# Modulation of layer 1 moved into the feed-forward, compression on shifted pairs in column strips, queries split once per half-row and copied by DMA

## The chip, the cores and the metric

The kernel runs on one core of a Trainium2 chip. The metric is the device time of one execution in microseconds; a time stands for the median of several runs. The profile is of one execution, whose span runs from its first to its last instruction.

## The reference, cut to what matters

Two layers over 1024 tokens of width 1024, float32. Each layer has a mixing sub-layer (four kinds of heads behind one input projection) and a feed-forward one; both are scaled and shifted by a modulation that depends on `c` alone.

```python
def reference(x, c, positions, ...):
    cond = jax.nn.silu(c)
    for l in range(DEPTH):
        mod = cond @ w_mod[l] + b_mod[l]
        sh1, sc1, gt1, sh2, sc2, gt2 = jnp.split(mod, N_MOD, axis=-1)
        h = rms_norm(x, norm_g[l, 0]) * (1.0 + sc1) + sh1
        y = mixer_block(h, positions, ...)
        x = x + gt1 * rms_norm(y, norm_g[l, 1])
        h = rms_norm(x, norm_g[l, 2]) * (1.0 + sc2) + sh2
        y = jnp.square(jax.nn.relu(h @ w_up[l])) @ w_down[l]
        x = x + gt2 * rms_norm(y, norm_g[l, 3])
    return x

# in the sparse attention of the mixer: 63 windows of 32 tokens, 16 apart, for keys (j=0) and values (j=1)
def compress(t, j):
    z = (t[:, blk] + cmp_pos[j]).reshape(B, n_cmp, CMP_BLOCK * HD)
    return jax.nn.silu(z @ cmp_w1[j]) @ cmp_w2[j]
```

The product `z @ w1` equals `t[blk] @ w1 + cmp_pos @ w1`, and the second term is the same for every window.

## The kernel before, in words

Tokens are worked on in two halves of T = 512, features on 128 partitions. The program calls, in this order: `mods_start` (load x, `cond` from c, the modulation j = 0 and 1 of layer 0), then for layer 0 `mix(0,0)`, `mix(0,1)`, `mods` for what is left, `ff(0,0)`, `mix(1,0)`, `ff(0,1)`, `mix(1,1)`, `ff(1,0)`, `ff(1,1)`. A scheduler reorders instructions within each engine by priority and readiness; the tail of a mixer half (residual and h2, under `tc.high_priority`) is put late. Every engine works its own list in order. All loads are issued by SP, in order, too.

**Matrix products.** A weight unit is 128x512 float32, 256 KB. It lands in a raw tile (`wraw`, L152), ACT casts it to the high part (L161), DVE subtracts to the low part (L125), and `mm3` (L167 to L169) makes three matmuls per 128 rows, 12 per unit. There are three lanes: `a` (3 raw tiles, 4 split ones), `b` (3 and 4) and `f` for the feed-forward (4 and 6, high and low each taking one). A feed-forward half has 128 units: `up` makes a hidden tile out of two (relu, square, split into `hid`), `down` one unit per output tile and group, summed into `y` by DVE (L131).

**Modulation.** `mod_col` takes one of 48 blocks of 128 outputs per layer: two 128x512 pieces of `w_mod` are loaded, each multiplied by `cond` and summed along the row by one DVE instruction with a read of its accumulator (L232), and both sums and the bias are added (L134). `mods_start` loads into 12 tiles `mw`; all the rest, 160 pieces, go through two tiles `mr` that belong to no stage, so the scheduler may place them anywhere from the first mixer on. Layer 0's j = 2 is due at the residual of `mix(0,0)`, j = 3 and 4 at its h2.

**Sparse attention** (`nsa_part`). `kvt` holds keys and values of the half with 16 columns of the half before. `compress` adds the positions into `zc` (8 DVE adds per call, L131), and multiplies by w1 in 32 matmuls (two passes each) that fill 32 of 128 output partitions (L650). A logistic chain on 32x256, two transposes and w2 give the compressed keys. Queries are rotated into `qr` and, for each block j of 128 tokens, split into a high and a low part (`qh`, L687, and `ql`, L125) that stand on both halves of the partitions: 4 casts and 4 subtractions. The scores (L744, L746) use them.

The GLA in the same mixer makes its state products on strips of 32 columns of the array:

```python
PE.matmul(kp[32 * hh:32 * hh + 32, j, :],
          k3t[64 * r:64 * r + 64, j, 32 * hh:32 * hh + 32],
          vtm[hh // 2][64 * r:64 * r + 64, j, 64 * (hh % 2):64 * (hh % 2) + 64],
          start=True, stop=True, tile_position=(64 * r, 32 * hh))
```

Of the kernel before, what the change touches and what calls it, by code (L numbers as in the profile page):

```python
# [7 lines left out]
F32 = mybir.dt.float32  # L8
# [8 lines left out]
DEPTH = 2  # L17
T = 512
# [17 lines left out]
def trunk_kernel(ctx, tc, xT, c, pos, freq, sel, w_in, conv_w, cmp_pos, cmp_w1, cmp_w2,  # L36
# [60 lines left out]
    par = []  # L97
    for l in range(DEPTH):
        d = {}
        for name, shape in (("ng", [128, 4, 8]), ("bmod", [128, 48]), ("conv", [128, 3, 2]),  # L100
                            ("pos", [128, 32]), ("gain", [128, 8]), ("mod", [128, 6, 8]),
                            ("A1", [128, 8]), ("G1", [128, 8]), ("A2", [128, 8]), ("G2", [128, 8])):
            d[name] = const.tile(shape, F32, name=f"{name}{l}")
        par.append(d)

    def load_params(l, names):
        src = {"ng": norm_g, "bmod": b_mod, "conv": conv_w, "pos": cmp_pos, "gain": gains}
        for n in names:
            dma(out=par[l][n], in_=src[n][l])

# [8 lines left out]
    cmp_halo = const.tile([128, 16], F32, name="cmp_halo")  # L119
# [108 lines left out]
    def mod_col(l, j, k, mk):  # L228
        mp = work.tile([128, 2], F32, name="mp", tag="mp", bufs=4)
        for kh in range(2):  # L230
            raw = mk(w_mod[l, 8 * j + k, :, kh * T:kh * T + T], [128, T])
            V.tensor_tensor_reduce(out=raw, in0=raw, in1=cond[kh], scale=1.0, scalar=0.0,  # L232
                                   op0=ALU.mult, op1=ALU.add, accum_out=mp[:, kh:kh + 1])
        stt(par[l]["mod"][:, j, k:k + 1], mp[:, 0:1], mp[:, 1:2], par[l]["bmod"][:, 8 * j + k:8 * j + k + 1],
            ALU.add, ALU.add)
# [332 lines left out]
    def nsa_part(l, hf, h, rg, gates):  # L568
# [65 lines left out]
        def compress():  # L634
            k4 = kvt.rearrange("p (a m r) -> p a m r", m=8, r=2)
            p4 = d["pos"].rearrange("p (b m r) -> p b m r", b=2, r=2)
            hid = ps("mm", (32, 2, 128))
            for jj in range(2):
                z = rg.tile([128, 16, 32], F32, name="zc", tag="P", bufs=3)
                rs = slice(64 * jj, 64 * jj + 64)  # L640
                for r in range(2):
                    for bb in range(2):
                        add(z[64 * r:64 * r + 64, 8 * bb:8 * bb + 8, :],
                            k4[rs, bb:bb + 32, :, r].rearrange("p a m -> p m a"),
                            p4[rs, bb, :, r:r + 1].to_broadcast([64, 8, 32]))
                for q in range(4):
                    w = bt((128, 4, 128))
                    dma(out=w, in_=cmp_w1[l, jj, :, 4 * q:4 * q + 4, :])
                    for m in range(4):
                        PE.matmul(hid[:, jj, :], z[:, 4 * q + m, :], w[:, m, :],  # L650
                                  start=(q == 0 and m == 0), stop=(q == 3 and m == 3))
            act = pt((32, 2, 128))
            logsig(act, hid, pt((32, 2, 128)))
            A.activation(act, act, AF.Exp)
            mul(act, act, hid)
# [21 lines left out]
        for j in range(4):  # L677
# [56 lines left out]
            # selected (every causal block) and window branches  # L734
# [59 lines left out]
            # compressed branch  # L794
# [39 lines left out]
    def mix(l, hf, h, between=None):  # L834
        d = par[l]
        gain = d["gain"]
        with ExitStack() as es:
            gr = es.enter_context(region("gates"))
            if l == 0 and hf == 0:
                sx = ("ff", "ff", "ff")  # L840
                with region("wb", "right") as lane_pool["b"]:
# [8 lines left out]
                    mods(0, (2, 3, 4))  # L850
# [32 lines left out]
    def ff(l, hf):  # L883
# [7 lines left out]
        def up(n):  # L891
# [9 lines left out]
            hid[n] = (hi, lo)  # L901

# [7 lines left out]
        def down(g, cs=slice(0, T), ws=None):  # L910
            for n in range(8):
# [151 lines left out]
```

## Time and profile before

| | |
|---|---|
| median of 3 runs | 2651.31 us (2650.48 to 2655.39) |
| profiled execution, span | 2656.2 us |
| PE busy | 2513.5 us, 95% |
| DVE busy | 1680.0 us, 63% |
| ACT busy | 1310.3 us, 49% |
| moved from and to HBM | 281.47 MB read, 17.83 MB written |
| mean granted clock of TensorE | 0.985 |

The span is 4.9 us above the median of the runs. PE is TensorE's matmuls, PEld its weight loads, DVE VectorE, ACT ScalarE, SP the engine that issues the DMAs. A share of busy time is a mean over all stages; a stage is read from its own stretch of the trace.

### The profile page before, as it was taken

The page shows a single profiled execution, that of the slowest core. Times are in us where ns is not written, and L with a number is a line of the kernel's source. Part 1 is how long each engine was busy: PE and PEld are TensorE (multiplying, and loading weights), DVE is VectorE, ACT ScalarE, POOL GpSimd, SP SyncE. Part 2 cuts the span into 40 slices and gives each one's busy share as a digit, 9 for nine tenths or more (in the row PEclk, how much of TensorE's full clock was granted, in tenths as well). Part 3 has the DMA queues.
Part 4 walks back from the last instruction along what each step waited for, and adds up shares of the span by engine and source line. Part 5 has one row for each costly group of instructions (what it writes and reads, how often), then busy time and mean ns, then how long its engine had stood idle before and what let it go on. Part 6 is the DMA issues. An engine that isn't in the chain of part 4 may idle for free.

```text
span 2656.2 us, 34273 instructions
## 1 busy us (share of the span) xinstructions
PE 2513.5 (95%) x11690; PEld 1989.3 (75%) x11690; DVE 1680.0 (63%) x3540; ACT 1310.3 (49%) x2649; POOL 56.5 (2%) x65
## 2 busy tenths in 40 slices
PE   2899879999999999999999999999999999999998
PEld 1676657677778887767788887777777888788887
DVE  7797987888574448457674446547876544534446
ACT  3474534468654345356653435345775443434343
POOL 0100000200000000010000000001000000000000
PEclk9999989999999999999999999999999999999999
DMA  7435566511343334222243334222123333533332
GB/s 270 138 97 174 192 204 202 179 53 36 100 142 98 96 99 143 82 71 69 95 144 100 96 97 145 88 61 89 40 76 121 98 96 99 179 97 98 96 99 84
DMA packets 168937, 301.56 MB, mean 114 GB/s; under 512 B 20453, under 2 KB 24122, under 8 KB 168762
## 3 DMA queue, kind: packets, MB, share of 16 engines
q1 hardware_dynamic: 168762, 299.37, 36.3%
q8 instruction: 92, 1.51, 0.2%
q14 instruction: 83, 0.68, 0.1%
HBM read 281.47 MB, written 17.83 MB: 113 GB/s over the span
## 4 chain that ended last, share of the span: by engine, by line
PE 76%; DVE 10%; ACT 4%; DMA 4%; issue 2%; POOL 0%; DVEq 0%; SPq 0%; ACTq 0%; POOLq 0%
PE ps_ff L168 16%; PE ps_ff L169 16%; PE ps_ff L167 16%; PE ps_mm L167 6%; PE ps_mm L169 6%; PE ps_mm L168 6%; DMA mr<-in_w_mod_dram 3%; PE ps_pv L705 1%; PE ps_pv L704 1%; DVE mr L232 1%; PE ps_mm L699 1%; ACT bp L754 1%; PE ps_t L189 1%; PE ps_s L744 1%; DVE w_a L125 1%
## 5 line engine op out<-in xcount | busy, mean ns | idle before, releaser
L161 ACT CAST w_f<-raw_f 128x512 fp32r<-128x512 f32 x504 | 313.3, 622 | 649.7 <-PE ps_ff L168 638.6
L125 DVE TENSOR_TENSOR w_f<-raw_f,w_f 128x512 fp32r<-128x512 f32 x504 | 348.7, 692 | 261.6 <-ACT w_f L161 254.7
L169 PE MATMUL ps_ff<-h,w_f 128*128 128x512 f32 x1024 | 405.9, 397 | 17.1 <-DVE w_f L125 17.1
L167 PE MATMUL ps_ff<-h,w_f 128*128 128x512 f32 x1024 | 404.8, 396 | 4.8 <-ACT h L203 4.8
L168 PE MATMUL ps_ff<-h,w_f 128*128 128x512 f32 x1024 | 406.6, 397 | 0.6 <-DVE h L134 0.4
L167 PE MATMUL ps_ff<-hid,w_f 128*128 128x512 f32 x992 | 388.9, 392 | 0.1
L168 PE MATMUL ps_ff<-hid,w_f 128*128 128x512 f32 x992 | 388.6, 392 | 0.0
L169 PE MATMUL ps_ff<-hid,w_f 128*128 128x512 f32 x992 | 388.2, 391 | 0.0
L167 PE MATMUL ps_mm<-h,w_a 128*128 128x512 f32 x832 | 336.4, 405 | 34.8 <-ACT w_a L161 30.5
L169 PE MATMUL ps_mm<-h,w_a 128*128 128x512 f32 x832 | 332.7, 400 | 11.7 <-DVE w_a L125 11.6
L168 PE MATMUL ps_mm<-h,w_a 128*128 128x512 f32 x832 | 338.8, 409 | 0.9 <-DVE h L125 0.9
L131 DVE TENSOR_TENSOR y<-y,ps_ff 128x512 f32<-128x512 f32 (+1 forms) x232 | 154.9, 668 | 238.0 <-PE ps_ff L169 237.1
L161 ACT CAST w_a<-raw_a 128x512 fp32r<-128x512 f32 x208 | 128.6, 618 | 233.0 <-PE ps_mm L168 216.2
L169 PEld LDWEIGHTS ps_ff<-h,w_f 128*128 128x128 f32 x1024 | 195.0, 190 | 60.1 <-DVE w_f L125 18.8
L125 DVE TENSOR_TENSOR w_a<-raw_a,w_a 128x512 fp32r<-128x512 f32 x208 | 143.3, 689 | 152.2 <-ACT w_a L161 146.0
L167 PEld LDWEIGHTS ps_ff<-h,w_f 128*128 128x128 f32 x1024 | 195.4, 191 | 47.6 <-ACT h L203 6.5
L168 PEld LDWEIGHTS ps_ff<-h,w_f 128*128 128x128 f32 x1024 | 195.0, 190 | 45.2 <-issue 2.7
L167 PEld LDWEIGHTS ps_mm<-h,w_a 128*128 128x128 f32 x832 | 158.0, 190 | 81.2 <-ACT w_a L161 33.6
L167 PEld LDWEIGHTS ps_ff<-hid,w_f 128*128 128x128 f32 x992 | 186.6, 188 | 40.5 <-issue 1.4
L168 PEld LDWEIGHTS ps_ff<-hid,w_f 128*128 128x128 f32 x992 | 186.7, 188 | 39.1 <-issue 1.0
L169 PEld LDWEIGHTS ps_ff<-hid,w_f 128*128 128x128 f32 x992 | 186.7, 188 | 37.8 <-issue 0.5
L169 PEld LDWEIGHTS ps_mm<-h,w_a 128*128 128x128 f32 x832 | 157.9, 190 | 55.8 <-DVE w_a L125 15.1
(350 smaller groups left out, 3586.4 us busy)
## 6 DMA issues: line engine op xcount, KB each, us to landing
raw_f<-in_w_up_dram SPq DMA_DIRECT2D x256, 256.0 KB, 2.7
raw_f<-in_w_down_dram SPq DMA_DIRECT2D x256, 256.0 KB, 2.6
mr<-in_w_mod_dram SPq DMA_DIRECT2D x160, 256.0 KB, 3.0
raw_a<-in_w_in_dram SPq DMA_DIRECT2D x144, 256.0 KB, 2.8
raw_a<-in_w_o_dram SPq DMA_DIRECT2D x64, 256.0 KB, 2.9
mw<-in_w_mod_dram SPq DMA_DIRECT2D x32, 256.0 KB, 4.4
bp<-in_cmp_w_dram SPq DMA_DIRECT2D x32, 256.0 KB, 4.6
raw_b<-in_w_in_dram SPq DMA_DIRECT2D x32, 256.0 KB, 3.0
```

The costliest lines, as they stand in the source:

```text
L125: V.tensor_tensor(out=out, in0=a, in1=b, op=ALU.subtract)
L131: eng.tensor_tensor(out=out, in0=a, in1=b, op=ALU.add)
L161: A.copy(hi, raw)
L167: PE.matmul(ps_ap, wh, xh, start=start, stop=False)
L168: PE.matmul(ps_ap, wh, xl, start=False, stop=False)
L169: PE.matmul(ps_ap, wl, xh, start=False, stop=stop)
L189: PE.matmul(p, ones, acc, start=True, stop=True)
L232: V.tensor_tensor_reduce(out=raw, in0=raw, in1=cond[kh], scale=1.0, scalar=0.0, op0=ALU.mult, op1=ALU.add, accum_out=mp[:, kh:kh + 1])
L699: PE.transpose(tp[0:kn, hh, :], cols(h0 + hh), ident)
L704: PE.matmul(pv[:, h0:h0 + nh, :], vst, th[0:kn], start=first[0], stop=False)
L705: PE.matmul(pv[:, h0:h0 + nh, :], vst, tl[0:kn], start=False, stop=last)
L744: PE.matmul(sp[:, 0:w], qh[:, h0 + hh, :], KX[:, 128 * k0:128 * k0 + w], start=True, stop=False)
```

## The change

Three things are done.

*Modulation.* `cond` becomes one 128x1024 tile, and a reduction may cover a whole block: `mod_dot` loads 512 KB and makes one 128x1024 reduction. The opening does 16 of these (6 tiles `mw`) and adds the bias for j = 0 and 1 at once. Layer 0's j = 2, 3, 4 stay in `mix(0,0)` as 48 pieces of 128x512 (`mod_half`), through the three raw tiles of lane `b`. The rest, 56 blocks, is handed to the feed-forward: `ff(0,0)` gets 48 and `ff(0,1)` 8, as steps that `up` and `down` call, with three tiles `mr` in a region `md` that lives as long as that feed-forward.

*Compression.* `kvt` holds two copies of each of keys and values, the second shifted by one token, on the two halves of the partitions, so that no `zc` is built. The 16 matmuls per part fill four strips of 32 columns in turn (`tile_position`), a matmul with `sel4` (four stacked 32x32 identities) sums the strips, and the positions' term is made once per layer in the same way and added on DVE. The logistic chain works on 128x64.

*Queries.* Each half-row of `qr` is split once, on its own partitions, and two DMAs per half (64 KB each) copy high and low part to the other half: 4 DMAs per block, 64 in all, on SP.

```diff
+    cond = const.tile([128, 1024], F32, name="cond")
+    def mod_dot(l, j, k, mk, acc):
+        raw = mk(w_mod[l, 8 * j + k], [128, 1024])
+        V.tensor_tensor_reduce(out=raw, in0=raw, in1=cond, scale=1.0, scalar=0.0,
+                               op0=ALU.mult, op1=ALU.add, accum_out=acc)
...
-                t = su.tile(shape, F32, name="mw", tag="mw", bufs=12)
+                t = su.tile(shape, F32, name="mw", tag="mw", bufs=6)
...
+                ma = work.tile([128, 2, 1], F32, name="ma", tag="ma", bufs=4)
                 for j in (0, 1):
-                    mod_col(0, j, k, mk)
+                    mod_dot(0, j, k, mk, ma[:, j, :])
+                add(par[0]["mod"][:, 0:2, k:k + 1], ma, bm[:, 0:2, k:k + 1])
...
-    def mods(l, js):
+    def mods_now(l, js, lane):
+        for j in js:
+            for k in range(8):
+                mod_half(l, j, k, lambda src, shape: wraw(lane, src, shape))
+            mod_scale(l, j, slice(0, 8))
+    def mods_steps(todo, pl):
         def mk(src, shape):
-            t = work.tile(shape, F32, name="mr", tag="mr", bufs=2)
+            t = pl.tile(shape, F32, name="mr", tag="mr", bufs=3)
             dma(out=t, in_=src)
             return t
-        for j in js:
+        for l, j in todo:
+            ma = work.tile([128, 8], F32, name="mv", tag="mv", bufs=2)
             for k in range(8):
-                mod_col(l, j, k, mk)
-            mod_scale(l, j, slice(0, 8))
+                mod_dot(l, j, k, mk, ma[:, k:k + 1])
+                if k == 7:
+                    add(par[l]["mod"][:, j, :], ma, par[l]["bmod"][:, 8 * j:8 * j + 8])
+                    mod_scale(l, j, slice(0, 8))
+                yield
...
-        kvt = rg.tile([128, 528], F32, name="kvt")
+        kvt = rg.tile([128, 2, 528], F32, name="kvt")
...
-        A.copy(kvt[:, 16:528], p)
+        for jj in range(2):
+            A.copy(kvt[0:64, jj, 16:528], p[64 * jj:64 * jj + 64])
+            V.tensor_copy(kvt[64:128, jj, 15:527], p[64 * jj:64 * jj + 64])
...
         def compress():
-            hid = ps("mm", (32, 2, 128))
-            for jj in range(2):
-                z = rg.tile([128, 16, 32], F32, name="zc", tag="P", bufs=3)
-                rs = slice(64 * jj, 64 * jj + 64)
-                for r in range(2):
-                    for bb in range(2):
-                        add(z[64 * r:64 * r + 64, 8 * bb:8 * bb + 8, :],
-                            k4[rs, bb:bb + 32, :, r].rearrange("p a m -> p m a"),
-                            p4[rs, bb, :, r:r + 1].to_broadcast([64, 8, 32]))
...
+            def partial(col):
+                hid = ps("mm", (128, 2, 128))
+                for jj in range(2):
+                    for i in range(16):
+                        c = i % 4
+                        PE.matmul(hid[32 * c:32 * c + 32, jj, :], col(jj, i), ws[4 * jj + i // 4][:, i % 4, :],
+                                  start=i < 4, stop=i >= 12, tile_position=(0, 32 * c))
+                hs = pt((128, 2, 128))
+                A.copy(hs, hid)
+                return hs
+            hx = partial(lambda jj, i: k5[:, jj, i // 8:i // 8 + 32, 2 * (i % 8)])
             hp_ = ps("mm", (128, 2, 32))
             for jj in range(2):
-                PE.transpose(hp_[:, jj, :], act[:, jj, :], ident[0:32, 0:32])
+                PE.matmul(hp_[:, jj, :], hx[:, jj, :], sel4, start=True, stop=True)
+            if hf == 0:
+                hb = partial(lambda jj, i: pos2[l][:, jj, 2 * i:2 * i + 32])
+                pb = ps("mm", (128, 2, 2))
+                for jj in range(2):
+                    PE.matmul(pb[:, jj, :], hb[:, jj, :], sel4[:, 0:2], start=True, stop=True)
+                A.copy(posb[l], pb[:, :, 0:1])
             hs = pt((128, 2, 32))
-            A.copy(hs, hp_)
+            add(hs, hp_, posb[l].to_broadcast([128, 2, 32]))
...
-                for o0 in (0, 64):
-                    V.tensor_copy(hv[o0:o0 + 64], qr[rs, :, tj])
-                for o0 in (0, 64):
-                    sub(lv[o0:o0 + 64], qr[rs, :, tj], hv[rs].bitcast(F32))
+                ro = slice(64 - 64 * r, 128 - 64 * r)
+                V.tensor_copy(hv[rs], qr[rs, :, tj])
+                sub(lv[rs], qr[rs, :, tj], hv[rs].bitcast(F32))
+                for v in (hv, lv):
+                    dma(out=v[ro].bitcast(F32), in_=v[rs].bitcast(F32))
...
-                    mods(0, (2, 3, 4))
+                    mods_now(0, (2, 3, 4), "b")
...
+    def ff(l, hf, todo=()):
+        if not todo:
+            return ff_body(l, hf, None)
+        with region("md") as rg:
+            steps = mods_steps(todo, rg)
+            y = ff_body(l, hf, lambda: next(steps, None))
...
             hid[n] = (hi, lo)
+            if step:
+                step()
...
                     add(y[n][:, cs], y[n][:, cs], p)
+                if step and n % 2:
+                    step()
...
-    mods(0, (5,))
-    mods(1, range(6))
-    xt = ff(0, 0)
+    xt = ff(0, 0, ((0, 5), (1, 1), (1, 0), (1, 2), (1, 4), (1, 3)))
...
-    xt = ff(0, 1)
+    xt = ff(0, 1, ((1, 5),))
```

**The order that comes out of it.** On SP in the tail of `mix(0,0)`, around the loads of the output projection's weights (`raw_a<-in_w_o`), before:

```order
L275 DMA mr<-in_w_mod_dram 128x512 x2
L152 DMA raw_f<-in_w_up_dram 128x512
L275 DMA mr<-in_w_mod_dram 128x512 x2
L152 DMA raw_a<-in_w_o_dram 128x512
L137 DMA xo<-in_xT_dram 128x512 x3
L152 DMA raw_a<-in_w_o_dram 128x512
L137 DMA xo<-in_xT_dram 128x512
L152 DMA raw_a<-in_w_o_dram 128x512
L275 DMA mr<-in_w_mod_dram 128x512 x2
L152 DMA raw_a<-in_w_o_dram 128x512
```

and now:

```order
L166 DMA raw_b<-in_w_in_dram 128x512 x11
L166 DMA raw_b<-in_w_mod_dram 128x512 x24
L151 DMA xo<-in_xT_dram 128x512
L166 DMA raw_a<-in_w_o_dram 128x512
L166 DMA raw_b<-in_w_mod_dram 128x512 x3
L166 DMA raw_a<-in_w_o_dram 128x512 x2
L166 DMA raw_b<-in_w_mod_dram 128x512 x3
L166 DMA raw_a<-in_w_o_dram 128x512
```

The loads of the modulation (`w_mod`) stood one or two at a time between the weight loads; now 24 in a row stand behind the last loads of lane `b` (`raw_b<-in_w_in`), and then threes between the weight loads. Five loads of `w_o` stand further up.

On SP in `ff(0,0)`, the loads of the feed-forward's weights (`raw_f`) before, of which there is nothing else in the list there:

```order
L152 DMA raw_f<-in_w_down_dram 128x512 x2
L152 DMA raw_f<-in_w_up_dram 128x512 x8
L152 DMA raw_f<-in_w_down_dram 128x512 x8
L152 DMA raw_f<-in_w_up_dram 128x512 x8
L152 DMA raw_f<-in_w_down_dram 128x512 x8
```

and now, a few units after the steps begin:

```order
L306 DMA mr<-in_w_mod_dram 128x1024 x3
L166 DMA raw_f<-in_w_up_dram 128x512
L306 DMA mr<-in_w_mod_dram 128x1024 x4
L166 DMA raw_f<-in_w_up_dram 128x512
L306 DMA mr<-in_w_mod_dram 128x1024 x3
L166 DMA raw_f<-in_w_up_dram 128x512
L306 DMA mr<-in_w_mod_dram 128x1024 x7
L166 DMA raw_f<-in_w_down_dram 128x512 x2
L306 DMA mr<-in_w_mod_dram 128x1024
```

Three to seven loads of 512 KB stand ahead of a weight load where none stood.

On DVE in `ff(0,0)`, before (`w_f` is a weight split, `y` the sum over groups, `hid` the split of a hidden tile):

```order
L125 TENSOR_TENSOR w_f<-raw_f,w_f 128x512
L131 TENSOR_TENSOR y<-y,ps_ff 128x512
L125 TENSOR_TENSOR w_f<-raw_f,w_f 128x512
L131 TENSOR_TENSOR y<-y,ps_ff 128x512
L125 TENSOR_TENSOR w_f<-raw_f,w_f 128x512
L125 TENSOR_TENSOR hid<-r,hid 128x512
L131 TENSOR_TENSOR y<-y,ps_ff 128x512
L125 TENSOR_TENSOR w_f<-raw_f,w_f 128x512 x3
```

and now (each `mr,mv` row is a 128x1024 reduction, the `mv` row behind it the read of its accumulator):

```order
L139 TENSOR_TENSOR w_f<-raw_f,w_f 128x512
L145 TENSOR_TENSOR mod_99<-mv,bmod_96 128x8
L247 ISA mr,mv<-mr,cond 128x1024
L247 ISA mv 128x1
L142 TENSOR_TENSOR G_103<-mod_99,ng_95 128x8
L139 TENSOR_TENSOR w_f<-raw_f,w_f 128x512 x2
L247 ISA mr,mv<-mr,cond 128x1024
L247 ISA mv 128x1
L247 ISA mr,mv<-mr,cond 128x1024
L247 ISA mv 128x1
L139 TENSOR_TENSOR w_f<-raw_f,w_f 128x512
```

One to three reductions stand ahead of each weight split. From the first of the 48 to the last the list holds 29 weight splits, and 30 of the reductions stand within the first 13 of these.

## Rows read from the trace of the kernel before

**Rows 1.** The first page: busy time by engine; shares of the last chain
```profile
PE 2513.5 (95%) x11690; PEld 1989.3 (75%) x11690; DVE 1680.0 (63%) x3540; ACT 1310.3 (49%) x2649; POOL 56.5 (2%) x65
...
PE 76%; DVE 10%; ACT 4%; DMA 4%; issue 2%; POOL 0%; DVEq 0%; SPq 0%; ACTq 0%; POOLq 0%
```

**Rows 2.** Table by stretch: length, busy by engine (count), clock, DMA share, GB/s
```profile
0.00:25.00 25.00, 2.07 (x2) 0.50 (x2) 17.85 (x54) 12.29 (x20) 1.50 (x9) 1.00 0.92 330
25.00:50.00 25.00, 1.02 (x3) 0.79 (x3) 24.50 (x73) 5.56 (x8) 0.00 (x0) 1.00 0.66 212
50.00:266.00 216.00, 201.30 (x1031) 149.62 (x1030) 172.20 (x512) 114.34 (x282) 13.48 (x14) 0.98 0.47 146
266.00:385.00 119.00, 95.27 (x355) 69.55 (x354) 107.61 (x232) 58.85 (x100) 0.72 (x1) 0.90 0.61 194
385.00:705.00 320.00, 305.47 (x1539) 231.65 (x1539) 259.54 (x659) 192.72 (x458) 13.86 (x13) 0.99 0.39 121
789.20:867.90 78.70, 78.70 (x349) 65.20 (x348) 33.25 (x51) 30.93 (x52) 0.00 (x0) 1.00 0.33 97
```

**Rows 3.** Timeline, DVE, opening: start, length, instruction
```profile
17.91 0.69 DVE L232 CUSTOM_DVE_ANT_0 mw<-mw,cond 128x512 f32<-128x512 f32 x1
18.52 0.22 DVE L134 SCALAR_TENSOR_TENSOR mod<-mp,bmod 128x1 f32<-128x1 f32 x1
18.65 0.69 DVE L232 CUSTOM_DVE_ANT_0 mw<-mw,cond 128x512 f32<-128x512 f32 x1
```

**Rows 4.** Groups by line and form: busy us, mean ns, idle before, its releaser
```profile
L232 DVE CUSTOM_DVE_ANT_0 mr<-mr,cond 128x512 f32<-128x512 f32 x160 | 110.6, 693 | 37.2 <-DMA mr<-in_w_mod_dram 36.6
...
L751 DVE CUSTOM_DVE_ANT_0 bp<-ps_s,cm 128x512 f32<-128x512 f32 x56 | 37.9, 685 | 2.6 <-PE ps_s L746 2.3
...
L650 PE MATMUL ps_mm<-bp,zc 128*32 128x128 f32 x256 | 31.4, 288 | 10.3 <-issue 10.3
...
L125 DVE TENSOR_TENSOR ql<-qr,qh 64x256 fp32r<-64x256 f32 x64 | 26.8, 418 | 1.4
...
L131 DVE TENSOR_TENSOR zc<-kvt,pos 64x256 f32<-64x256 f32 x32 | 22.9, 753 | 0.3
...
L687 DVE CAST qh<-qr 64x256 fp32r<-64x256 f32 x64 | 18.4, 288 | 2.3 <-PE ps_s L765 0.8 <-PE ps_s L744 0.3
...
L751 DVE CUSTOM_DVE_ANT_0 bp<-ps_s,cm 128x128 f32<-128x128 f32 x24 | 6.5, 285 | 3.0 <-PE ps_s L746 2.8
```

**Rows 5.** Instructions on mr in 50 to 266, 266 to 385, 385 to 705
```profile
L232 DVE CUSTOM_DVE_ANT_0 mr<-mr,cond x55: 647/686/1152, 82.2 to 265.7; 128x512 f32<-128x512 f32 x55
L232 DVE CUSTOM_DVE_ANT_0 mr<-mr,cond x42: 679/685/693, 265.7 to 382.6; 128x512 f32<-128x512 f32 x42
L232 DVE CUSTOM_DVE_ANT_0 mr<-mr,cond x64: 671/691/1200, 385.3 to 544.5; 128x512 f32<-128x512 f32 x64
```

**Rows 6.** Timeline, PE, around the compression: start, length, [idle before, releaser]
```profile
99.21 0.60 PE L650 MATMUL ps_mm<-bp,zc 128*32 128x128 f32 x2 [4.34 <-issue]
...
532.27 0.38 PE L650 MATMUL ps_mm<-bp,zc 128*32 128x128 f32 x2 [1.99 <-issue]
...
544.53 0.50 PE L744 MATMUL ps_s<-KS,qh 128*128 128x512 f32 x1 [2.59 <-ACT bp L758]
```

**Rows 7.** DMA issues: KB each, median us from issue to landing
```profile
mr<-in_w_mod_dram SPq DMA_DIRECT2D x160, 256.0 KB, 3.0
...
raw_a<-in_cmp_w_dram SPq DMA_DIRECT2D x4, 64.0 KB, 2.5
```

**Rows 8.** Timeline, PE and PEld, strips of the GLA in mix(0,1)
```profile
463.21 0.40 PE L169 MATMUL ps_mm<-h,w_a 128*128 128x512 f32 x1
463.54 0.65 PE L500 MATMUL ps_t<-g 64*32 64x64 f32 x32
464.12 0.50 PE L167 MATMUL ps_mm<-h,w_a 128*128 128x512 f32 x1
...
463.54 0.49 PEld L500 LDWEIGHTS ps_t<-g 64*32 64x32 f32 x32 [0.37 <-ACT g L493]
```

More of the change, by code (lines that the diff above doesn't have):

```diff
@@ L106, in load_params @@
     def load_params(l, names):
-        src = {"ng": norm_g, "bmod": b_mod, "conv": conv_w, "pos": cmp_pos, "gain": gains}
+        src = {"ng": norm_g, "bmod": b_mod, "conv": conv_w, "gain": gains}
         for n in names:
-            dma(out=par[l][n], in_=src[n][l])
+            if n == "pos":
+                for jj in range(2):
+                    rows = slice(64 * jj, 64 * jj + 64)
+                    dma(out=pos2[l][0:64, jj, 0:32], in_=cmp_pos[l, rows, :])
+                    dma(out=pos2[l][64:128, jj, 0:31], in_=cmp_pos[l, rows, 1:32])
+            else:
+                dma(out=par[l][n], in_=src[n][l])
     KS = const.tile([128, 1024], F32R, name="KS")
@@ L118, in trunk_kernel @@
     conv_halo = const.tile([128, 2, 2], F32, name="conv_halo")
-    cmp_halo = const.tile([128, 16], F32, name="cmp_halo")
+    cmp_halo = const.tile([128, 2, 16], F32, name="cmp_halo")
+    pos2 = [const.tile([128, 2, 64], F32, name=f"pos2{l}") for l in range(DEPTH)]
+    posb = [const.tile([128, 2, 1], F32, name=f"posb{l}") for l in range(DEPTH)]
+    sel4 = const.tile([128, 32], F32, name="sel4")
+    for l in range(DEPTH):
+        V.memset(pos2[l], 0.0)
+    V.tensor_tensor(out=sel4, in0=ident[:, 0:32], in1=ident[:, 32:64], op=ALU.add)
+    for q in (2, 3):
+        V.tensor_tensor(out=sel4, in0=sel4, in1=ident[:, 32 * q:32 * q + 32], op=ALU.add)
     st_carry = const.tile([128, 64], F32, name="st_carry")
@@ L231, in mod_col @@
             raw = mk(w_mod[l, 8 * j + k, :, kh * T:kh * T + T], [128, T])
-            V.tensor_tensor_reduce(out=raw, in0=raw, in1=cond[kh], scale=1.0, scalar=0.0,
+            V.tensor_tensor_reduce(out=raw, in0=raw, in1=cond[:, kh * T:kh * T + T], scale=1.0, scalar=0.0,
                                    op0=ALU.mult, op1=ALU.add, accum_out=mp[:, kh:kh + 1])
@@ L255, in mods_start @@
                 t1, t2 = (su.tile([128, T], F32, name="ct", tag="ct", bufs=4) for _ in range(2))
-                dma(out=cond[hf], in_=c[:, hf * T:hf * T + T].to_broadcast([128, T]))
-                logsig(t2, cond[hf], t1)
+                ch = cond[:, hf * T:hf * T + T]
+                dma(out=ch, in_=c[:, hf * T:hf * T + T].to_broadcast([128, T]))
+                logsig(t2, ch, t1)
                 A.activation(t2, t2, AF.Exp)
-                mul(cond[hf], cond[hf], t2)
+                mul(ch, ch, t2)
             xt = load_x(0)
@@ L648, in compress @@
                     dma(out=w, in_=cmp_w1[l, jj, :, 4 * q:4 * q + 4, :])
[L649 to L655, printed above, removed]
+                    ws.append(w)
+            def partial(col):
[9 more added lines that the diff above has]
+            hx = partial(lambda jj, i: k5[:, jj, i // 8:i // 8 + 32, 2 * (i % 8)])
             hp_ = ps("mm", (128, 2, 32))
             for jj in range(2):
-                PE.transpose(hp_[:, jj, :], act[:, jj, :], ident[0:32, 0:32])
-            hs = pt((128, 2, 32))
-            A.copy(hs, hp_)
+                PE.matmul(hp_[:, jj, :], hx[:, jj, :], sel4, start=True, stop=True)
+            if hf == 0:
+                hb = partial(lambda jj, i: pos2[l][:, jj, 2 * i:2 * i + 32])
+                pb = ps("mm", (128, 2, 2))
+                for jj in range(2):
+                    PE.matmul(pb[:, jj, :], hb[:, jj, :], sel4[:, 0:2], start=True, stop=True)
+                A.copy(posb[l], pb[:, :, 0:1])
+            hs = pt((128, 2, 32))
+            add(hs, hp_, posb[l].to_broadcast([128, 2, 32]))
+            act = pt((128, 2, 32))
+            logsig(act, hs, pt((128, 2, 32)))
+            A.activation(act, act, AF.Exp)
+            mul(hs, hs, act)
             kc = ps("mm", (128, 2, 64))
@@ L881, in mix, with ff_body @@
         return res
-    def ff(l, hf):
+    def ff(l, hf, todo=()):
[4 more added lines that the diff above has]
+            y = ff_body(l, hf, lambda: next(steps, None))
+            assert next(steps, 0) == 0
+            return y
+    def ff_body(l, hf, step):
         d = par[l]
```

17 lines of the change are left out of this document (9 added, 8 removed).

## The prediction

> **What bounds the kernel.** The first page says TensorE: it is busy 95% of the span, VectorE 63%, and the chain that ended last runs 76% through PE and 10% through DVE [rows 1]. Such shares average stages with different limits, so the table by stretch comes next [rows 2]. Up to 50 us PE does almost nothing (2.07 and 1.02 us) while DVE is busy 17.85 and then 24.50 of 25: the opening is DVE's. From 50 to 266 PE is busy 201.30 of 216.00, so 14.7 are idle; from 266 to 385, the tail of the first mixer half, 95.27 of 119.00 at a granted clock of 0.90, with DVE at 107.61; from 385 to 705, 305.47 of 320.00. The feed-forward stretch 789.20 to 867.90 has PE at 78.70 of 78.70 and DVE at 33.25: there PE alone bounds, with 45 us of DVE to spare. The change takes DVE work from the first three stretches and puts most of it into the last kind.
>
> The profiled execution has a span of 2656.2 us, 4.9 above the median of 2651.31; the sum is made on the span and carried to the median as a difference. About 0.2%, 5.3 us, is what a measurement of this kernel tells from no change.
>
> **Prices.** One 128x512 reduction lasts 0.69 us, but the next thing starts 0.61 us later (17.91, 18.52), the accumulator read lying inside; the scalar add behind a pair moves the next start by 0.13 (18.52, 18.65) [rows 3]. I use 0.61 for any 512-wide DVE operation in a row. A 1024-wide one stands nowhere. The same kind of operation on the scores takes 285 ns for 128 columns and 685 for 512 [rows 4], 1.04 ns a column, so 512 more columns add 0.53: 1.14 in a row, at most 0.69 + 0.53 + 0.08 = 1.30 with nothing overlapped. I take 1.14, since the opening shows that rhythm for the same operation.
>
> **Opening.** 32 x 0.61 + 16 x 0.13 = 21.6 becomes 16 x 1.14 + 8 x 0.13 = 19.3: **2.3 gained** (at 1.30, 0.2 lost). Only DVE works there, so it counts in full.
>
> **Modulation leaves the mixers.** 55 reductions start in 50 to 266, 42 in 266 to 385, 64 in 385 to 705 [rows 5] (one on an edge counts twice; there are 160). The first and the last group go, some 34 and 39 us of DVE. Of PE's idle time there, 14.7 + 14.5 = 29.2, the compression's gaps are 4.34, 1.99 and 2.59 [rows 6], and 20.3 is left. No row says how many of those waits end with DVE freed; I take half: **10 gained** (5 to 18).
>
> **The tail of mix(0,0).** Layer 0's j = 2, 3, 4 stay, now in the three raw_b tiles. In the new order 47 reductions fall between the end of the conv and the end of the tail, where the table has 42, and 24 of their loads stand on SP ahead of the sixth w_o load, where only a few stood ahead of each. That tail is DVE's (107.61 of 119.00): 5 x 0.61 = 3. The 24 loads turn in three tiles; with 3.0 us of landing [rows 7] and 0.61 of use, (3.0 + 0.61) / 3 = 1.2 each, 29 us in all. The five w_o units ahead, 14 us of PE, and the waits before them, in which the loads already turn, cover most of that; I add 3. **6 lost** (0 to 15).
>
> **ff(0,0).** The code calls for one reduction per two weight units, but the order shows another thing: all 48 stand within 29 units, 30 of them within the first 13. A unit is 78.70 / 29 = 2.71 us of PE. First part: DVE has 30 x 1.14 + 22 x 0.61 (13 weight splits, 5 sums, 4 hidden splits) = 47.6 us against 13 x 2.71 = 35.2 of PE. Second part: 18 x 1.14 + 28 x 0.61 = 37.6 against 43.4, so nothing is lost. The six w_f tiles are three units, two ahead of PE: 5.4 us of cover. From DVE alone the loss is 47.6 - 35.2 - 5.4 = 7. Then the loads: SP has three or more 512 KB loads ahead of each weight load. 256 KB land in 3.0 us; 256 KB more at the 330 GB/s of the opening [rows 2] are 0.8, so 3.8, and three tiles give (3.8 + 1.14) / 3 = 1.65 each, 49.4 us for 30. If none of DVE's other work fits into those waits, the first part is 49.4 + 13.4 = 62.8 and the loss 22, with 18 x 1.65 + 17.1 - 43.4 = 3 more in the second part: 25. The nearest row is the wait of today's 160 reductions with two tiles, 36.6 us in all [rows 4], 0.23 each; 30 x 0.23 = 7 on top of the 7 gives **14 lost** (7 to 25). PE's gaps of 1 to 2 us may also lower its clock; where DVE sets the pace this costs little.
>
> **ff(0,1).** Eight reductions, 9.1 us of DVE, stand right after h2 of mix(1,0) where weights of the next units queue behind them; 5.4 of cover: **3 lost** (0 to 8).
>
> **Compression.** L650 is 31.4 us of PE in four calls, 7.85 each, with 10.3 idle just before them [rows 4]. The GLA's matmuls on 32-column strips show the new form: 32 passes of 64 columns between the starts 463.54 and 464.12, 18 ns each; entering costs 0.10 us (0.33 from 463.21 to 463.54, against 2.71 / 12 = 0.23 for a 512-column matmul), and I count as much for leaving [rows 8]. With 128 columns I double it: 64 x 36 ns + 0.2 = 2.5 per call. Saved 4 x 5.3 = 21; the positions' pass costs 2 x 2.5 = 5, the sums over strips about 1: 15. DVE loses 32 zc adds of 0.75, 32 casts of 0.29 and 32 subs of 0.42 [rows 4], 47 us, and gains 8 copies, about 5. The first scores wait for this work: a gap of 2.59 at 544.53 [rows 6], with the 10.3 some 13, smaller ones not counted. The copies by DMA come in between: the nearest row, 64 KB, has 2.5 us to landing [rows 7]. They start right after DVE's four splits instead of eight and run beside the strips, so I take 7 of 13. **22 gained** (0 to 30). The later blocks' copies are issued while another block is worked on; that is their cover, and the third rival is what it costs without it.
>
> The 64 new issues on SP stand in front of weight loads that have three or four tiles of lead: nothing. POOL is unchanged.
>
> **A rule against the strips.** The weight loads of the GLA's strips run 32 in 0.49 us, 15 ns each [rows 8], so they overlap too. The Trainium skill, "TensorEngine Tiling (Array Packing)", section Restrictions, says that column tiling switches off fast weight load. By it the loads could become the bound and the strips bring nothing; the row speaks against that, and it is a rival below.
>
> **Sum.** 2.3 + 10 - 6 - 14 - 3 + 22 = 11.3 gained: 2656.2 - 11.3 = 2644.9 on the span, 2651.3 - 11.3 = **2640.0** for the median.
>
> **Rivals.**
> First, ff(0,0) absorbs its reductions and the mixers gain fully: a loss of 7 instead of 14, 18 gained instead of 10. For it: 45 us of DVE spare in the feed-forward; against it: 47.6 over 35.2. 2640 - 7 - 8 = 2625. Chance 0.18.
> Second, on the other side: the loads starve PE. SP issues in order, so a weight load waits behind a modulation load that waits for its tile, and DVE, in order too, holds the weight splits behind a reduction whose data is late. At the upper end of both ff terms (25 and 8) and of the tail (15) it is 11 + 5 + 9 = 25 more: 2665; with the feed-forward alone 2656. It decides when all of it costs over 39 us instead of 23. For it: three of every four loads in that order; against it: 0.23 us of wait per reduction now. Chance 0.20.
> Third, the query copies are late: twelve later blocks (three in each of four calls) wait half a landing, 1.25 us, and the 7 of gaps is not got: 15 + 7 more, 2662. For it: 64 issues on one queue among weight loads; against it: splits stand a block ahead. Chance 0.13.
> Fourth, the strips run one after the other, bound by their weight loads, at the pace of now: 21 not saved and 2 x 5.3 more for the positions, 2640 + 32 = 2672. Against it stand 18 ns a pass. Chance 0.04. (The page's rule would lead here.)
> The forecast itself, 2630 to 2650, has 0.42; other mishaps 0.03.
>
> **Chances.** Faster by over 0.2% (below 2646): 0.34 of the forecast's 0.42 and the first rival, 0.52. Within (to 2656.6): 0.08, 0.05 of the second, 0.05 of the third, 0.02 of the rest, 0.20. Slower: 0.28. The range, 2620 to 2665, leaves out the fourth rival, the worst of the second and the best of the first. The forecast's own range is 2630 to 2650.
>
> **What would show it.** Right: PE idle in 50 to 266 and 385 to 530 down by half; L650's successor at some 2.5 us a call; PE idle of 10 to 20 us in one stretch of some 90 us of ff(0,0), waiting for weight splits, and full PE before and after it. Wrong: that stretch longer than 110 us or without a gap, reductions idle for their DMA well over 0.23 us each, score matmuls idle for DMA of qh or ql, or strip passes at 110 ns.

## The result, and the profile after

The change is slower: 2678.43 us against 2652.6 of the kernel before in the same comparison, ratio 1.0095 (95% interval 1.0081 to 1.0109), where 2640.0 was forecast, at most 2665. The profiled execution has a span of 2675.8 us, 19.6 above the one of before: of the 25.8 us between the medians the traces place 19.6, and where the rest lies no trace shows.

First page of the changed kernel, busy time and shares of the last chain:

```profile
PE 2512.1 (94%) x11834; PEld 1975.5 (74%) x11834; DVE 1625.8 (61%) x3264; ACT 1311.6 (49%) x2657; POOL 52.8 (2%) x65
...
PE 80%; DVE 6%; DMA 5%; ACT 4%; issue 2%; POOL 0%; SPq 0%; DVEq 0%; ACTq 0%; POOLq 0%
```

TensorE is busy as long as before (2512.1 against 2513.5 us in [rows 1]); VectorE is busy 54 us less. So in the balance the 20 us are PE's waiting. But the product with w1 alone takes 19.7 us less of PE (below), so other matmuls took longer, and both have to be found by place. For that the two traces are laid side by side: the start of the same matmul (the n-th of lane a, b or f) in both, and the difference. The table is worked out from the timelines; positive is later than before. The last four columns are experiments told of below. The rows are places at which both kernels have done the same matmuls of all three lanes, but for at most five of the feed-forward (1.1 us) at 386.4 and 1976.3. Elsewhere a difference can mislead: at 1298.9, inside mix(1,0), it is 20.2, with 13 matmuls of the feed-forward (3 us) still to do that the kernel before had done.

```
                              before   change  e_early  e_gate2  e_best2  e_m
opening, first lane a           49.0     +1.6     +1.0     +1.0     +1.0   +0.6
end of the conv, mix(0,0)      271.1     -0.6     +5.1     +1.3     +6.5   +0.6
behind the tail of mix(0,0)    386.4    +14.8     -1.9    +16.6     -0.9  +18.1
end of mix(0,1), in ff(0,0)    785.7     -2.1    -18.5     +0.1    -19.3   +4.8
60 us on, in ff(0,0)           845.5    +27.2    +11.2     +0.1    -19.3  +37.5
end of ff(0,0)                1026.6    +27.2    +11.6     +0.1    -19.3  +37.5
behind mix(1,0), in ff(0,1)   1335.6    +23.1     +8.5     -5.6    -24.0  +35.8
ff(0,1)                       1408.2    +25.9    +12.8     -4.3    -23.9  +40.0
mix(1,1)                      1976.3    +19.9     +8.8     -9.8    -28.5  +39.9
ff(1,1)                       2594.4    +19.8    +10.0     -8.8    -27.7  +39.5
```

So the mixers gain (2.2 up to the conv, 16.9 in mix(0,1), 4.1 and 6.0 in layer 1: 29.2 in all), and four places lose: 1.6 in the opening, 15.4 in the tail of mix(0,0), 29.3 in ff(0,0) within 60 us of the old time, 2.8 in ff(0,1): 49.1.

Table by stretch of the changed kernel, columns as in [rows 2]:

```profile
0.00:50.60 50.60, 2.08 (x2) 0.50 (x2) 39.72 (x90) 18.14 (x28) 1.50 (x9) 1.00 0.82 277
50.00:266.00 216.00, 203.07 (x1105) 151.67 (x1106) 129.51 (x358) 115.75 (x286) 12.36 (x14) 0.96 0.27 83
266.00:401.20 135.20, 100.00 (x363) 71.05 (x362) 112.44 (x246) 59.45 (x100) 0.97 (x1) 0.85 0.58 186
784.00:872.80 88.80, 68.29 (x264) 53.38 (x263) 71.93 (x124) 21.51 (x37) 0.00 (x0) 0.87 0.86 293
822.00:848.00 26.00, 10.81 (x33) 7.18 (x32) 18.27 (x34) 4.83 (x8) 0.00 (x0) 0.72 0.86 297
```

In the kernel before as many matmuls, 264, take the stretch of the first line; the second is of the changed kernel, four microseconds behind PE's longest wait:

```profile
784.00:843.50 59.50, 59.50 (x264) 49.27 (x263) 25.96 (x40) 20.72 (x35) 0.00 (x0) 1.00 0.34 101
```

```profile
848.00:852.00 4.00, 3.99 (x9) 3.10 (x10) 3.29 (x7) 1.24 (x2) 0.00 (x0) 0.50 0.97 347
```

So the 29.3 us lost are of two kinds. PE waits 20.5 us (it is busy 68.29 of 88.80), and 264 matmuls of the same kind keep it busy 68.29 us instead of 59.50, 8.8 more, since its granted clock is at 0.87 on the mean, at 0.72 in the worst 26 us, and at 0.50 (1.2 of 2.4 GHz) in those four. The DMAs, at 101 GB/s there before, run at 293. The tail now ends 15.4 us later than it did, counted from the end of the conv.

PE's longest waits in the tail and in ff(0,0), from its timeline (start, length, instruction, [idle before and what ended it]):

```profile
372.37 1.22 PE L203 MATMUL ps_t<-nt,ones 128*128 128x512 f32 x1 [16.76 <-DVE nt L145]
...
806.25 0.70 PE L183 MATMUL ps_ff<-h,w_f 128*128 128x512 f32 x1 [4.39 <-DVE w_f L139]
...
827.77 0.80 PE L181 MATMUL ps_ff<-h,w_f 128*128 128x512 f32 x1 [3.75 <-ACT w_f L175]
...
848.01 0.80 PE L181 MATMUL ps_ff<-hid,w_f 128*128 128x512 f32 x1 [10.29 <-ACT w_f L175]
```

Who ACT and DVE wait for from 784 to 873 (waiting, for what: us in total, times, longest):

```profile
ACT w_f L175 <- DMA raw_f<-in_w_up_dram: 13.1, 4, 5.5
ACT w_f L175 <- DMA raw_f<-in_w_down_dram: 9.7, 2, 8.3
```

```profile
DVE mr L247 <- DMA mr<-in_w_mod_dram: 10.5, 13, 1.9
```

PE's own waits in the same stretch, and SP's list ahead of the longest of them (start, length, what is issued):

```profile
PE ps_ff L181 <- ACT w_f L175: 15.2, 3, 10.3
PE ps_ff L183 <- DVE w_f L139: 5.3, 2, 4.4
```

```profile
828.13 0.37 SPq L166 DMA_DIRECT2D raw_f<-in_w_up_dram  x1
830.21 12.05 SPq L306 DMA_DIRECT2D mr<-in_w_mod_dram  x7
842.36 0.86 SPq L166 DMA_DIRECT2D raw_f<-in_w_down_dram  x2
```

ACT stands 22.8 us at weight units that have not landed, DVE 10.5 us at reductions whose block has not. Both engines and SP work their lists in order, so each such wait holds up whatever stands behind it: seven blocks take SP 12.05 us between two weight loads, ACT waits 8.3 us for what the later one brings, and PE 10.3 us for ACT. Of PE's 20.5 us of waiting 15.2 come this way, through the loads, and 5.3 from weight splits that stand behind reductions on DVE.

Groups and DMA issues of the changed kernel that answer to [rows 4] and [rows 7]:

```profile
L247 DVE CUSTOM_DVE_ANT_0 mr<-mr,cond 128x1024 f32<-128x1024 f32 x56 | 68.1, 1223 | 16.8 <-DMA mr<-in_w_mod_dram 16.2
...
L255 DVE CUSTOM_DVE_ANT_0 raw_b<-raw_b,cond 128x512 f32<-128x512 f32 x48 | 32.2, 688 | 5.5 <-DMA raw_b<-in_w_mod_dram 4.7
...
L689 PE MATMUL ps_mm<-bp,kvt 128*32 128x128 f32 x256 | 11.7, 296 | 5.1 <-DMA bp<-in_cmp_w_dram 5.1
```

```profile
mr<-in_w_mod_dram SPq DMA_DIRECT2D x56, 512.0 KB, 4.8
...
qh<-qh SPq DMA_DIRECT2D x32, 64.0 KB, 2.1
```

The 512 KB land in 4.8 us, not 3.8. The w1 product is 11.7 us of PE in four calls and 5.1 idle, against 31.4 and 10.3.

### The profile page after: what moved, and what is told of

Same layout as the page of the kernel before. It is cut to its first block, busy times and chain, and to the rows that moved or that the text cites. A ratio compares the mean times of both kernels' runs of the same rounds, so it can differ in the third digit from the quotient of the medians.

```text
span 2675.8 us, 34402 instructions
## 1 busy us (share of the span) xinstructions
PE 2512.1 (94%) x11834; PEld 1975.5 (74%) x11834; DVE 1625.8 (61%) x3264; ACT 1311.6 (49%) x2657; POOL 52.8 (2%) x65
## 4 chain that ended last, share of the span: by engine, by line
PE 80%; DVE 6%; DMA 5%; ACT 4%; issue 2%; POOL 0%; SPq 0%; DVEq 0%; ACTq 0%; POOLq 0%
PE ps_ff L181 16%; PE ps_ff L183 16%; PE ps_ff L182 16%; PE ps_mm L181 7%; PE ps_mm L183 7%; PE ps_mm L182 7%; PE ps_pv L756 1%; PE ps_pv L755 1%; DMA mr<-in_w_mod_dram 1%; DMA raw_b<-in_w_mod_dram 1%; PE ps_s L795 1%; PE ps_mm L750 1%; PE ps_t L203 1%; PE ps_s L797 1%; PE ps_t L750 1%
## 5 line engine op out<-in xcount | busy, mean ns | idle before, releaser
L183 PE MATMUL ps_ff<-h,w_f 128*128 128x512 f32 x1024 | 406.9, 398 | 19.7 <-DVE w_f L139 19.7
L181 PE MATMUL ps_ff<-hid,w_f 128*128 128x512 f32 x992 | 389.7, 393 | 11.5 <-ACT w_f L175 10.3
```

What stands on the lines that cost most here:

```text
L181: PE.matmul(ps_ap, wh, xh, start=start, stop=False)
L183: PE.matmul(ps_ap, wl, xh, start=False, stop=stop)
```

## Experiments

**One tile mr, and layer 0's reductions earlier.** Two kernels, each against one of the two big losses.

```diff
-            t = pl.tile(shape, F32, name="mr", tag="mr", bufs=3)
+            t = pl.tile(shape, F32, name="mr", tag="mr", bufs=1)
```

> The change with one tile mr instead of three, so that the list of DVE holds the 48 reductions of ff(0,0) over 75 weight units instead of 29; nothing else moves. Packing theory: the 29 us that TensorE loses between 784 and 873 us of the changed kernel come from 37 reductions and their 512 KB loads within 22 weight units; spread out, under 6 us are lost there, and the median is 2649 to 2660 (from 2678.4). Rival: a reduction of 1024 columns costs the feed-forward about 0.6 us wherever it stands (its load delays the weight loads): the median stays at 2670 or above.

Measured: ratio 1.0037 (1.0022 to 1.0051), 0.58% better than the change and between both expectations. In ff(0,0) PE loses 2.8 us in the 60 us where the change lost 29.3, but 15.6 in all, in small pieces up to 1030 us. Waits of DVE, then of PE, from 784 to 1044 us of this kernel:

```profile
DVE mr L247 <- DMA mr<-in_w_mod_dram: 76.1, 47, 2.6
```

```profile
PE ps_ff L181 <- DVE y L145: 9.3, 9, 1.6
```

With a single tile each of the 47 reductions waits 1.6 us for its block, and the sums of the feed-forward behind it wait too, until PE lacks a PSUM tile. So packing is not the only way to lose time: a block that is late for its reduction costs too.

In `wunit`, and where the GLA begins (`mods_now` is a generator here that yields behind each block):

```diff
+        if lane == "b":
+            next(bsteps[0], None)
...
+                        bsteps[0] = mods_now(0, (2, 3, 4), "b")
                         ol = gla_part(l, hf, h, rg, "b", sx, lrT)
```

> The change with layer 0's j = 2, 3, 4 made one block (two reductions of 512 columns) behind each weight unit of lane b instead of all behind the last unit. Theory: the tail of mix(0,0) loses 16 us because 45 reductions instead of 24 stand before the residual on DVE; with them gone from there the residual starts at 325 to 340 us instead of 357, and the median falls by 14 to 26, to 2652 to 2664. Rival: the tail is a chain of norms whatever DVE has ahead of it, or the loads then delay the gemms of lane b by as much: 2672 to 2682.

Measured: 1.0040 (1.0025 to 1.0054), 0.55% better, at the near end of what the theory had. The first scaling of the residual on DVE, in the kernel before, in the change and in this one:

```profile
339.55 1.41 DVE L134 SCALAR_TENSOR_TENSOR yo<-yo,G,nt 128x512 f32<-128x512 f32 x2
```

```profile
357.03 1.42 DVE L148 SCALAR_TENSOR_TENSOR yo<-yo,G,nt 128x512 f32<-128x512 f32 x2 [2.00 <-ACT nt L208]
```

```profile
340.19 1.42 DVE L148 SCALAR_TENSOR_TENSOR yo<-yo,G,nt 128x512 f32<-128x512 f32 x2 [0.40 <-ACT nt L211]
```

It starts 17 us later in the change and is back with the reductions gone from ahead of it; they cost 5.7 us up to the conv instead.

**The parts alone.** Kernel before with the modulation's hunks of the diff only (all on `cond`, `mod_dot`, `mods_now`, `mods_steps`, `ff`), and with the queries' hunk only:

```diff
-                for o0 in (0, 64):
-                    V.tensor_copy(hv[o0:o0 + 64], qr[rs, :, tj])
...
+                V.tensor_copy(hv[rs], qr[rs, :, tj])
...
+                    dma(out=v[ro].bitcast(F32), in_=v[rs].bitcast(F32))
```

> Kernel before with the modulation's part of the change alone (wide reductions, lane b, steps in the feed-forward); compression and queries as before. If compression and queries gain the 20 us or so that the lags in mix(0,0) to mix(1,1) suggest, this kernel is slower than the change: 2692 to 2704. Rival: they gain nothing and the mixers' gain is the moved modulation's: 2675 to 2682.

Measured: 1.0151 (1.0135 to 1.0168). Compression and queries together are worth 0.56% within the change, 15 us. The table shows the modulation alone losing 17.5 in the tail and 33 in ff(0,0).

> Kernel before with the queries' part alone: split once per half-row, copied by DMA. Theory: DVE gets 23 us of work less and the copies land in 2.1 us beside other work: 2 to 6 us faster than before, 2646 to 2651. Rival (third of the prediction): the copies are late for the later blocks: 5 to 12 us slower, 2657 to 2664.

Measured: 0.9997 (0.9984 to 1.0010): no difference, neither of the two. Up to the conv it loses 7.4 us, in the later mixers it gains as much.

**Modulation bound to its steps.** So that blocks land early and reductions still stand apart, a DVE operation on one column of the tile reads the step's own result ahead of each reduction; three tiles.

```diff
         raw = mk(w_mod[l, 8 * j + k], [128, 1024])
+        if g is not None:
+            stt(raw[:, 0:1], g, 0.0, raw[:, 0:1], ALU.mult, ALU.add)
...
-                step()
+                step(r[:, 0:1])
```

> The change with three tiles mr again, and a DVE operation on one column ahead of each reduction that reads the hidden or output tile of its step, so that a reduction cannot be placed before its step: on DVE's list one stands per two weight units, over 90 units, and its load is issued a step or more earlier. Theory: of the 15 us that one tile mr still cost, all was DVE standing at a reduction whose load had not landed (1.1 to 2.0 us each time) while sums of the feed-forward wait behind it; loaded ahead, the 48 cost under 5 us between 784 and 1060 us, and the median is 2648 to 2656. Rival: the reduction's own 1.2 us delays the sums and PE waits for the PSUM tile: 10 us or more are lost there, 2660 to 2668.

Measured: 1.0600 (1.0583 to 1.0618), a miss of the experiment's own making. Stretch 550 to 760 of this kernel:

```profile
550.00:760.00 210.00, 149.53 (x634) 105.20 (x634) 146.00 (x343) 127.72 (x312) 0.00 (x0) 0.85 0.15 49
```

The change has PE at 209.44 of 210 there, since feed-forward units fill the mixer's waits. Here the step of the first hidden tile cannot run before the region `md` has its memory, which mix(0,1) still holds: the first reduction starts at 762 us. Until then the step keeps the only tile `r`, and every unit behind stands: PE starts the sixth weight unit of the feed-forward at 544 us and the seventh at 762, where the change has started 27 by 686. The kernel with both edits fell with it:

> Both: layer 0's reductions spread over lane b, layer 1's bound to their steps in the feed-forward, three tiles mr. If both losses are independent, the lag behind the kernel before stays near -15 us from 750 us on: 2625 to 2640, faster than both kernels. Rival: what is saved in the first half comes back at a later wait (the feed-forward's DVE, the tail of mix(0,1)): 2645 to 2655.

Measured: 1.0540 (1.0520 to 1.0560).

**Loads alone, reductions alone.** To see which of the two starves PE in ff(0,0): first n = 64 with all loads, then (below the dots) no loads with all columns, for the feed-forward's reductions only. Both kernels leave out part of the sums, and each ran once, so they are read by place alone.

```diff
-        V.tensor_tensor_reduce(out=raw, in0=raw, in1=cond, scale=1.0, scalar=0.0,
+        V.tensor_tensor_reduce(out=raw[:, 0:n], in0=raw[:, 0:n], in1=cond[:, 0:n], scale=1.0, scalar=0.0,
...
-            dma(out=t, in_=src)
-        V.tensor_tensor_reduce(out=raw, in0=raw, in1=cond, scale=1.0, scalar=0.0,
+        V.tensor_tensor_reduce(out=raw, in0=raw if ld else cond, in1=cond, scale=1.0 if ld else 1e-4, scalar=0.0,
```

> The change with the 56 reductions of the feed-forward over 64 of 1024 columns (the rest of the sum is left out); all loads stay. DVE's list holds 24 of them within 4 weight units, so the loads stand closer still. If the loads starve PE (the weight loads behind them on SP and in the DMA queues), PE loses 20 us or more between 784 and 873 us. If DVE's own time was the cause, under 6.

> The change with the 56 reductions of the feed-forward taken of cond instead of a loaded tile (their weights are left out, and their loads); DVE's time stays. 23 stand in a row on DVE's list ahead of one weight split, and the rest within 19 units. If DVE's time is the cause, PE loses 15 to 25 us there (23 x 1.15 us less some 5 to 8 us of cover); if the loads are, under 6.

Measured by the same table of starts: 33.3 us lost with loads alone, 25.3 with reductions alone; the change lost 29.3. Waits of ACT in the first, of PE in the second:

```profile
ACT w_f L175 <- DMA raw_f<-in_w_up_dram: 36.6, 2, 35.0
```

```profile
PE ps_ff L181 <- DVE y L145: 23.0, 1, 23.0
```

In the first ACT waits 35 us for one weight unit, behind 25 blocks in SP's list; in the second PE waits 23 us for a sum of the feed-forward that stands behind 22 reductions. Either alone is enough. How much of the change's 29.3 belongs to which these two do not tell, since their lists are packed more tightly than the change's (at most seven blocks in a row); the waits above do, for PE's waiting. The 25 blocks took SP 42.36 us, 1.69 each, with reductions of 64 columns, and the change's seven 1.72 each, so it is not the reductions that set the blocks' pace there. That the place in the lists costs, and not the amount of data or of work, is what the next experiment is for.

**Steps from the fifth group on.** The gated form once more, started when the region is free, gated by tiles that are not alone.

```diff
-                if live[0]:
+                if live[0] and n >= 4 * G:
...
-                step(r[:, 0:1])
+                step(n, lo[:, 0:1].bitcast(F32))
...
-                if step and n % 2:
-                    step()
+                if step and g:
+                    step(G * g + G, y[n][:, 0:1])
```

> As the gated kernel before, with the steps starting at the fifth of eight groups of the feed-forward (their region of SBUF is free by then, so no hidden tile is held up), and one step per hidden tile and per output tile: on DVE's list the 48 stand over 62 weight units, after the 62nd, and loads are issued two or three steps ahead. Theory (packing and late loads are the loss): under 6 us lost in ff(0,0) instead of 29, under 3 in ff(0,1) instead of 6, so 22 to 29 us faster than the change: ratio to before 0.998 to 1.002. Rival (a reduction in the list of the feed-forward costs the sums behind it 0.2 us or more each): 10 us or more lost, ratio above 1.003.

Measured: 0.9969 (0.9958 to 0.9980), better than the range given. From 785.7 to 1026.6 of the old time nothing is lost at all, and in ff(0,1) 1.3 instead of 2.8. Stretch and waits of DVE:

```profile
784.00:1030.00 246.00, 243.25 (x1069) 200.03 (x1067) 181.20 (x338) 98.53 (x163) 0.63 (x1) 1.00 0.66 213
```

```profile
DVE mr L148 <- DMA mr<-in_w_mod_dram: 3.6, 11, 0.8
```

The same 48 reductions and blocks: 213 GB/s where the change's packed stretch has 293, and 3.6 us of DVE waiting for blocks where that stretch has 10.5. So it was the place that cost. This edit and the earlier reductions of layer 0 together:

> Gated steps as in the kernel beside it, and layer 0's reductions behind the weight units of lane b. If both losses are independent the ratio to before is 0.990 to 0.996, faster than both kernels (the one kernel gained 0.55% of the change's 0.95% loss with lane b alone). Rival: 0.998 or above.

Measured: **0.9918** (0.9905 to 0.9930), 2633.5 us, faster than both kernels. The two losses are independent: 0.51% between this kernel and the last is what 0.55% was before.

**The queries once more**: that hunk taken back, in the last kernel and in the change.

> The kernel beside it without the queries' part (casts and subtractions as before, no copies by DMA). If the copies bring nothing on balance (alone they made no difference: 0.9997), within 0.15% of the kernel beside it. If the DVE work that they save counts once the mixers are free of modulation, 0.2% or more slower; if their landing is waited for, 0.2% or more faster.

Measured: 0.9943 (0.9930 to 0.9957): without the queries' part 0.25% slower, 6.6 us.

> The change without the queries' part. The same question beside the modulation as it is in the change: within 4 us of the change's ratio 1.0095 if the copies bring nothing on balance; 1.011 or above if the saved DVE work counts, 1.007 or below if the landings are waited for. With the kernel that has modulation alone (1.0151) the difference is what the compression brings: 10 to 15 us.

Measured: 1.0118 (1.0105 to 1.0132): 0.23% slower, 6 us; the compression is the other 0.33%, 9 us, just under what was expected. Queries alone brought nothing beside the old compression (whose 8 adds stood ahead of them on DVE and whose product PE had to wait for) and the old place of the modulation, and 6 us once both had changed. Which of the two makes the difference no run shows.

## Why the prediction was wrong

Its sum was 34.3 gained and 23 lost; measured 29.2 gained and 49.1 lost. The gains were nearly right in size, in part by luck (see the mixers); the losses were put at less than half. The second rival had the right mechanism, and its upper ends for the three places that lose (15, 25 and 8: 48 us) come close to the 47.5 measured. Its 2665 is still short, as the opening did not gain and the mixers gained a little less. None of the signs that the prediction named for being wrong showed (the stretch in ff(0,0) is 88.8 us, a reduction waits 0.28 us for its block, no score waits for a copy, a strip pass takes 26 ns): they did not watch what failed.

- **Opening**: 2.3 gained was forecast, 1.6 lost. The price was right, 1.14 us from a reduction's start to what follows it, and DVE begins its last two scalings of the opening at 45.15 us instead of 47.48, 2.3 earlier, as forecast. The step that failed is "only DVE works there, so it counts in full": now the first weight unit is what comes last. SP issues its load at 45.47 instead of 44.73 us, behind eight loads of the positions where there were two, and ACT waits 4.17 us for it. Reduction and its read in the changed kernel, then ACT's first weight cast before and now:

```profile
16.68 1.22 DVE L247 CUSTOM_DVE_ANT_0 mw<-mw,cond 128x1024 f32<-128x1024 f32 x1
17.82 0.08 DVE L247 DVE_READ_ACCUMULATOR2_ANT ma<- 128x1 f32 x1
```

```profile
48.31 0.62 ACT L161 CAST w_a<-raw_a 128x512 fp32r<-128x512 f32 x1 [0.20 <-DMA raw_a<-in_w_in_dram]
```

```profile
49.95 1.27 ACT L175 CAST w_a<-raw_a 128x512 fp32r<-128x512 f32 x2 [4.17 <-DMA raw_a<-in_w_in_dram]
```

- **Tail of mix(0,0)**: 6 lost (0 to 15) against 15.4. The step that failed is "47 reductions fall between the end of the conv and the end of the tail, where the table has 42": a count over the tail. What counts is how many stand ahead of the residual on DVE, since the residual, its norm and h2 are one chain and PE waits for it: 45 against 24. 21 x 0.65 (the mean from one to the next) = 14, and the order had it. Reductions between the end of the conv and the residual, before and now:

```profile
L232 DVE CUSTOM_DVE_ANT_0 mr<-mr,cond x24: 682/686/693, 272.8 to 338.2; 128x512 f32<-128x512 f32 x24
```

```profile
L255 DVE CUSTOM_DVE_ANT_0 raw_b<-raw_b,cond x45: 680/691/695, 271.0 to 336.1; 128x512 f32<-128x512 f32 x45
```

- **ff(0,0)**: 14 lost (7 to 25) against 29.3. The step that failed is the price of the loads: the point of the sum takes DVE's own wait, 0.23 us a reduction, and a weight load that stands on SP behind the blocks has no term but the upper end. DVE's wait came out near that, 10.5 us for the 38 reductions there, 0.28 each. The weight loads behind the blocks cost ACT 22.8 us and, through ACT, PE 15.2; the 1.72 us a block is close to the upper end's 1.65, though a block lands in 4.8 us, not 3.8. The mean over 13 units with 5.4 us of cover also hid something: in DVE's list 24 reductions stand within 8 units, 24 x 1.14 + 15 x 0.61 = 36.5 us of DVE against 22 of PE. The 20.5 us of waiting alone lie inside the range; the slower matmuls come on top. "PE's gaps of 1 to 2 us may also lower its clock; where DVE sets the pace this costs little": the gaps are up to 10.3 us, the matmuls take 8.8 us more, and of these 3.0 are lost for certain: behind the last wait PE waits for nothing more, and at the lower clock it falls from 24.2 to 27.2 us behind. How much of the other 5.8 would have been waiting anyway is not known.
- **ff(0,1)**: 3 (0 to 8) against 2.8, as forecast; with the steps bound it is 1.3.
- **Mixers**: 10 was forecast for modulation gone, 22 for compression and queries; the parts alone give 15 for compression and queries, and the rest of the 29.2, some 14, goes to the modulation (the modulation alone gains 13.3 in mix(0,1), from +18.1 to +4.8). The split was off in both terms, in opposite directions; that the total is near is luck.
- **Strips**: forecast 2.5 us a call; measured 11.7 in four, 2.9 each, since three of the calls are broken into rounds between other matmuls (the unbroken one takes 1.98). One record lasts 0.27 and eight in a row 0.45, so (0.45 - 0.27) / 7 = 26 ns a pass, under the 36 taken. The fourth rival is out. What was late next is w1's load, 5.1 us of PE. A strip round of mix(1,0), and the matmul behind it:

```profile
1235.17 0.45 PE L689 MATMUL ps_mm<-bp,kvt 128*32 128x128 f32 x8
1235.55 0.50 PE L181 MATMUL ps_ff<-h,w_f 128*128 128x512 f32 x1
```

- **The rule on strips** (the Trainium skill, "TensorEngine Tiling (Array Packing)", Restrictions: column tiling switches off fast weight load): the trace does not show it to cost anything. The weight loads of the product lasted 138 ns in the median where they were 110 on L650, but those of the positions' pass, on the same strips, last 110. What differs is that the columns of `kvt` are read 16 apart and those of `pos` side by side; that this makes the 28 ns is argued, not tested. Either way the loads run side by side and a pass takes 26 ns:

```profile
L689 PEld LDWEIGHTS ps_mm<-bp,kvt x256: 131/138/166, 94.7 to 1848.9; 128*32 128x32 f32 x128
L689 PEld LDWEIGHTS ps_mm<-bp,pos x128: 106/110/110, 98.0 to 1240.9; 128*32 128x32 f32 x128
```

- **Late copies**: they land in 2.1 us, and in the changed kernel no wait of PE is ended by one. The third rival is out.
- **That the edit does not spread the steps** was seen in the order and told; its price was not.

## What to carry to other kernels

Work that nothing waits for is placed by the list as soon as its memory is free, all of it at once; in engines and queues that run in order it then stands ahead of work that everything waits for. Moving it into a stage with 45 us to spare per 79 is not enough: bind each piece to a step of that stage, with its load a step or more ahead and by a tile that nothing else lacks. And count what moves by the place of the next chain that starts behind it, not by the stretch.

## What the runs showed of the hardware that was not expected

A 512 KB block took 3.6 us to land in the median with one tile, 4.2 with three and reductions that stand apart, and 4.8 in the change. A copy of 64 KB from SBUF to SBUF took 2.1; the 64 KB load took 2.5 before [rows 7] and 1.7 in the changed kernel, so it is neither clearly more nor less. A 32-column strip pass of 128 columns took 26 ns side by side with three others, though its weight load alone lasts 138, or 110 where the columns lie side by side. Behind a wait of 10.3 us PE ran at a granted clock of 0.50 (848 to 852 us), a matmul of 512 columns every 0.43 us instead of 0.23.
